# NSA attention: the compressed branch's values in two matmuls and a bank of their own, added to the stored unit by GpSimd

## The chip, the cores and the metric

The kernel runs on one core of one Trainium2 chip. The metric is the device time of one execution in microseconds (us); a change of a few microseconds in some 2300 is looked for. The engines are named as in the profile: PE is TensorE (PEld its weight loads), DVE is VectorE, ACT is ScalarE, POOL is GpSimd, SP is SyncE. Each of them takes its instructions from a queue in a fixed order; semaphores order them against each other.

## The reference

The program is a decoder trunk of four layers on 512 tokens of width 1024: RG-LRU, native sparse attention (NSA), gated linear attention, RG-LRU, each followed by a SwiGLU network. All is float32. The change concerns the NSA layer alone, and in it the sum over three branches at the end:

```
p_c = masked_softmax(lg_c, dist_c >= 0)                      # compressed branch: 31 blocks of keys
o_c = jnp.einsum('bghqn,bngd->bqghd', p_c.astype(vc.dtype), vc)
...
return gi[..., 0:1] * o_c + gi[..., 1:2] * o_s + gi[..., 2:3] * o_w
```

There are 16 heads in 4 groups; a group shares its keys and values, a head has 64 dimensions, and a block of queries has 128 tokens, so there are 4 groups times 4 query blocks = 16 pairs (g, i). Each query sees three branches: compressed (o_c), selected (o_s; with 512 tokens all blocks are selected) and window (o_w).

## The kernel before

The attention stage (function attention, from L957) runs over 32 units: a unit is a group g, a block of queries i and a branch br (0: selected and compressed together, 1: window). The order of the blocks within a group is in NSA_AT["order"]. run() (L1159) steps over the units: it issues the logits of the unit three steps ahead (L1005), some filler matmuls (queries of the last group, and later the output product of the first two groups, L1074), the multiplications of the unit after that by its softmax weights on GpSimd (weights, L1054, the multiply is L1060), and then the values of the present unit (L1086).

In values, the exponentials of each head are transposed by PE into a bank "pt" (L1116) and copied or split from PSUM to SBUF by ScalarE and VectorE (L357 and L358, or L1120, L1122); the product with the values V is accumulated over all key blocks of both branches in one PSUM bank "ob" per pair (g, i) (L1103 to L1106). The products are queued in pend and come out up to four steps late (drain). For the compressed branch, the weights of four heads stand in one 128x128 tile (four heads times 32 blocks): PE transposes it (L1095), ScalarE copies it into the slot pc (L1097), and four matmuls (L1109), one a head, each with the 64 value columns of that head in vcd (zero outside the head's 32 rows), add to the lower 64 partitions of ob.

When the window branch of a pair is finished, store() (L1130) reads ob twice for each of two half rows (ScalarE copies L1136, VectorE adds L1137), which gives the unit's output ov in a slot "o"; then ScalarE and VectorE split it into a high and a low part for the output product (L1143, L1144). The output product of groups 0 and 1 is filler within the attention, that of groups 2 and 3 follows after it (output(4), L329 to L331 with tile "no").

PE's queue in the attention is in the order in which the program is written (manual_schedule). The order of the other engines is made by a planner when the kernel is built: it simulates, with its own costs, which instruction is ready when, and takes the earliest in program order of those ready. PSUM has 8 banks in one pool (bank()); the small SBUF tiles are 54 slots of 128x512 in one pool (slot()). A tile waits until the tile that had its place before has been read for the last time. GpSimd also issues the DMAs that add one weight block to another (L250, L293), in the same queue as its arithmetic.

Of the kernel before, what the change touches and what calls it, by code (L numbers as in the profile page):

```python
# [11 lines left out]
AF = mybir.ActivationFunctionType  # L12
OP = mybir.AluOpType
# [179 lines left out]
class Kernel:  # L193
# [762 lines left out]
    def attention(self, j, kc, kw, qw, V, vcd, gt, os, queries, output):  # L956
        nc, mm = self.nc, self.nc.tensor.matmul  # L957
# [33 lines left out]

        small = lambda s, n=4: self.fixed.tile([128, n], F32, name=self.name(s), tag=s, bufs=4)
        lag, depth = NSA_AT["lag"][0], NSA_AT["depth"][0]
        st, OB, pend, stored = {}, {}, [], []
        LC = [self.fixed.tile([128, 128], F32, name=f"lc{i}") for i in range(4)]
        for x in LC:
            nc.gpsimd.memset(x, 0.0)
# [72 lines left out]
        def drain(n):  # L1070
            while len(pend) > n:
                pend.pop(0)()
# [13 lines left out]
        def values(u, es):  # L1086
            g, i, br = u
            d = st.pop(u)
            L = d["L"]
            if br == 0:  # L1090
                OB[g, i] = self.bank("ob")
            ob = OB[g, i]
            if br == 0:
                b = self.bank("pc")
                nc.tensor.transpose(b[:, 0:128], d["lc"][:, 0:128], self.ident)  # L1095
                pc = self.slot("pc")
                nc.scalar.activation(pc[:, 0:128], b[:, 0:128], AF.Copy)  # L1097

            def product(jt, p):
                v = V[jt, br][:, g * 128:g * 128 + 128]  # L1100
                first, last = br == 0 and jt == 0, br == 1 and jt == i
                if len(p) == 1:
                    mm(ob, lhsT=v.bitcast(F32), rhs=p[0], start=first, stop=last)  # L1103
                else:
                    mm(ob, lhsT=v, rhs=p[0], start=first, stop=False)
                    mm(ob, lhsT=v, rhs=p[1], start=False, stop=last)  # L1106
                if br == 0 and jt == 0:
                    for hh in range(4):
                        mm(ob[0:64, hh * 128:hh * 128 + 128], lhsT=vcd[:, g, hh, :], rhs=pc[:, 0:128], start=False, stop=False)  # L1109

            ne = len(es)
            for jt in range(i + 1):
                b = self.bank("pt")
                for hh in range(4):
                    c = slice(hh * 128, hh * 128 + 128)
                    nc.tensor.transpose(b[:, c], L[hh][:, jt * 128:jt * 128 + 128], self.ident)  # L1116
                if NSA_AT["whole"][g] >> (jt + 4 * br) & 1:
                    p = [self.slot("p")]
                    if (jt + br) % 2:
                        nc.scalar.activation(p[0], b, AF.Copy)  # L1120
                    else:
                        nc.vector.tensor_copy(p[0], b)  # L1122
                else:
                    p = self.split(b, "p")
                pend.append(lambda jt=jt, p=p: product(jt, p))
                drain(depth)
                for _ in range(ne * (jt + 1) // (i + 1) - ne * jt // (i + 1)):
                    es.pop(0)()
            if br == 1:
                def store():  # L1130
                    o = self.slot("o")
                    ov = o[:, 0:256].rearrange("p (b n) -> p b n", n=128)
                    obv = ob.rearrange("p (b two n) -> p b two n", b=2, two=2)
                    for e in range(2):
                        me, ot = slice(e * 64, e * 64 + 64), slice(64 - e * 64, 128 - e * 64)
                        nc.scalar.activation(ov[me], obv[ot, :, e], AF.Copy)  # L1136
                        nc.vector.tensor_tensor(ov[me], obv[me, :, e], ov[me], op=OP.add)  # L1137
                    for b in range(2):
                        k = 2 * g + b
                        if k not in os:  # L1140
                            os[k] = (self.slot("oh", F32R), self.slot("ol", F32R))
                        hi, lo = (t[:, i * 128:i * 128 + 128] for t in os[k])
                        nc.scalar.activation(hi, ov[:, b], AF.Copy)  # L1143
                        nc.vector.tensor_tensor(lo, ov[:, b], hi.bitcast(F32), op=OP.subtract)  # L1144
                    stored.append(u)
                pend[-1] = lambda f=pend[-1]: (f(), store())
# [12 lines left out]
        def run():  # L1159
            for n in range(-lag, N):  # L1160
                es = []
                if n + lag < N:
                    logits(units[n + lag])
                    es = st[units[n + lag]]["exp"]
                fill(NSA_AT["fill"][n % 8])
                if 0 <= n + lag - 1 < N:
                    weights(units[n + lag - 1])
                if n >= 0:
                    values(units[n], es)
                while es:  # L1170
                    es.pop(0)()
                fill(NSA_AT["more"][n % 8] if n >= 1 else NSA_AT["start"][0])
                k = (n + lag) % 8
                if n + lag < 24:
                    for x, t in enumerate(NSA_AT["prep"]):
                        if t == k:
                            prep(units[n + lag][0] + 1, x)
            drain(0)
            for _ in work:
                pass  # L1180
# [290 lines left out]
```

## Time and profile before

| | us |
|---|---|
| median of 3 runs | 2312.25 (2311.42 to 2312.82) |
| the profiled execution's own time | 2310.41 |
| its span, first to last instruction | 2308.7 |
| attention stage in the trace | about 664 to 852 |

Over the span PE is busy 2277.9 us (99%), DVE 1482.1 (64%), ACT 1221.8 (53%) and POOL 346.9 (15%). A share of busy time is a mean over stages that have different limits; the stage around the change has to be read for itself. PE's busy time is modelled with overlapping ends, so a busy PE is not one at its peak. Matmuls on plain float32 appear as two instructions each.

### The profile page before, as it was taken

What the parts mean: (1) busy time and instruction counts of PE and PEld (TensorE: products, weight loads), DVE (VectorE), ACT (ScalarE), POOL (GpSimd) and SP (SyncE); (2) the same over time, 40 slices, a digit from 0 to 9 for tenths busy, and PEclk for the clock granted to TensorE, in tenths of its full rate; (3) what the DMA queues carried; (4) which work ended last, traced back from release to release, by engine and by line L of the source; (5) the groups of instructions that cost most, each with busy time, mean ns of one, the idle gap of its engine ahead of it and who ended that gap; (6) DMA issues with size and microseconds to landing.
All of it is one profiled execution on the core that took longest, in us unless ns stands there. A gap on an engine that the chain in (4) does not pass through costs nothing.

```text
span 2308.7 us, 29405 instructions
## 1 busy us (share of the span) xinstructions
PE 2277.9 (99%) x10898; PEld 1913.5 (83%) x10898; DVE 1482.1 (64%) x2460; ACT 1221.8 (53%) x1971; POOL 346.9 (15%) x413
## 2 busy tenths in 40 slices
PE   8999999999999999999999999999999999999998
PEld 7877888898876778888998887888898887888897
DVE  7887646466289888555466536745466786745555
ACT  5965535353468766444455435625354685635353
POOL 1001101001356531010110000101010000201010
PEclk9999999999999999999999999999999999999999
DMA  9246857452531137666673223958485224857561
GB/s 285 88 119 174 208 133 197 105 151 91 169 83 28 47 87 198 171 151 173 133 218 98 82 74 110 218 137 187 128 201 168 93 79 134 215 147 179 142 140 68
DMA packets 99455, 323.84 MB, mean 140 GB/s; under 512 B 11248, under 2 KB 18032, under 8 KB 99312
## 3 DMA queue, kind: packets, MB, share of 16 engines
q1 hardware_dynamic: 70512, 225.49, 28.9%
q0 software_dynamic: 28800, 96.48, 24.2%
q8 instruction: 85, 1.39, 0.2%
q14 instruction: 58, 0.48, 0.1%
HBM read 316.68 MB, written 5.24 MB: 139 GB/s over the span
## 4 chain that ended last, share of the span: by engine, by line
PE 86%; DVE 8%; ACT 4%; issue 1%; POOL 0%; DMA 0%; SPq 0%; POOLq 0%; DVEq 0%; ACTq 0%
PE pj L330 9%; PE pj L331 9%; PE pj L329 9%; PE b L592 8%; PE b L593 8%; PE b L591 8%; PE t L592 3%; PE t L593 3%; PE t L591 3%; PE lp L329 2%; PE lp L331 2%; PE lp L330 2%; PE at L663 2%; DVE ws L288 1%; DVE L L1032 1%
## 5 line engine op out<-in xcount | busy, mean ns | idle before, releaser
L288 DVE TENSOR_TENSOR ws<-wr,ws 128x1024 fp32r<-128x1024 f32 (+1 forms) x402 | 474.8, 1184 | 414.2 <-ACT ws L287 411.4
L287 ACT ACTIVATE ws<-wr 128x1024 fp32r<-128x1024 f32 (+1 forms) x402 | 409.7, 1021 | 494.0 <-PE pj L331 215.3
L330 PE MATMUL pj<-al,ws 128*128 128x512 f32 (+1 forms) x728 | 278.7, 383 | 0.0
L329 PE MATMUL pj<-ah,ws 128*128 128x512 f32 (+1 forms) x728 | 278.7, 384 | 0.0
L331 PE MATMUL pj<-ah,ws 128*128 128x512 f32 (+1 forms) x728 | 278.4, 382 | 0.0
L288 DVE TENSOR_TENSOR ws<-wc,ws 128x1024 fp32r<-128x1024 f32 (+1 forms) x144 | 163.2, 1133 | 134.7 <-ACT ws L287 133.3
L287 ACT ACTIVATE ws<-wc 128x1024 fp32r<-128x1024 f32 (+1 forms) x144 | 142.2, 988 | 129.2 <-PE pj L331 70.9
L330 PEld LDWEIGHTS pj<-al,ws 128*128 128x128 f32 x728 | 136.9, 188 | 27.1 <-DVE al L358 1.1
L331 PEld LDWEIGHTS pj<-ah,ws 128*128 128x128 f32 x728 | 136.8, 188 | 26.4
L329 PEld LDWEIGHTS pj<-ah,ws 128*128 128x128 f32 x728 | 136.9, 188 | 26.1
L293 POOL DMA_DIRECT2D wc<-wall x88 | 80.4, 923 | 439.6 <-DVE ws L288 431.6
L250 POOL DMA_DIRECT2D wc<-wall x64 | 57.6, 900 | 572.8 <-DMA wc<-wall 231.6
L591 PE MATMUL b<-ws,ph 128*128 128x512 f32 (+1 forms) x384 | 143.4, 373 | 0.0
L592 PE MATMUL b<-ws,xh 128*128 128x512 f32 (+1 forms) x384 | 142.7, 372 | 0.0
L593 PE MATMUL b<-ws,xl 128*128 128x512 f32 (+1 forms) x384 | 142.4, 371 | 0.0
L593 PE MATMUL b<-ws,pl 128*128 128x512 f32 (+1 forms) x384 | 142.4, 371 | 0.0
L592 PE MATMUL b<-ws,ph 128*128 128x512 f32 (+1 forms) x384 | 142.4, 371 | 0.0
L591 PE MATMUL b<-ws,xh 128*128 128x512 f32 (+1 forms) x384 | 142.4, 371 | 0.0
L329 PE MATMUL lp<-xh,ws 128*128 128x512 f32 x320 | 126.1, 394 | 6.6 <-ACT ws L287 6.6
L331 PE MATMUL lp<-xh,ws 128*128 128x512 f32 x320 | 124.4, 393 | 1.1 <-DVE ws L288 1.1
L330 PE MATMUL lp<-xl,ws 128*128 128x512 f32 x320 | 125.4, 392 | 0.0
L541 DVE TENSOR_TENSOR h<-h,pj 128x512 f32<-128x512 f32 x116 | 77.4, 683 | 36.3 <-PE pj L331 36.3
(374 smaller groups left out, 5233.0 us busy)
## 6 DMA issues: line engine op xcount, KB each, us to landing
wr<-wall SPq DMA_DIRECT2D x322, 512.0 KB, 4.2
wc<-wall POOLq DMA_DIRECT2D x104, 512.0 KB, 7.1
wc<-wall SPq DMA_DIRECT2D x40, 512.0 KB, 3.9
wc<-wall POOLq DMA_DIRECT2D x48, 384.0 KB, 6.1
wr<-wall SPq DMA_DIRECT2D x48, 384.0 KB, 3.2
wr<-wall POOLq DMA_DIRECT2D x32, 512.0 KB, 6.2
wc<-wall SPq DMA_DIRECT2D x16, 384.0 KB, 3.1
wr<-wall POOLq DMA_DIRECT2D x16, 384.0 KB, 6.2
```

Source lines behind the costliest of these rows:

```text
L250: self.nc.gpsimd.dma_start(self.raw[i][:, 0:n], self.wall[b][:, 0:n], accum_op=OP.add)
L287: self.nc.scalar.activation(hi, r, AF.Copy)
L288: self.nc.vector.tensor_tensor(lo, r, hi.bitcast(F32), op=OP.subtract)
L293: self.nc.gpsimd.dma_start(whole[:, 0:n], self.wall[self.uses[on][2][0]][:, 0:n], accum_op=OP.add)
L329: mm(ps, lhsT=wh, rhs=x[0], start=first, stop=False)
L330: mm(ps, lhsT=wh, rhs=x[1], start=False, stop=False)
L331: mm(ps, lhsT=wl, rhs=x[0], start=False, stop=last)
L541: nc.vector.tensor_tensor(self.h[m + c], self.h[m + c], banks[c], op=OP.add)
L591: mm(o, lhsT=xh, rhs=wh, start=first and k == 0, stop=False, skip_group_check=True)
L592: mm(o, lhsT=xh, rhs=wl, start=False, stop=False, skip_group_check=True)
L593: mm(o, lhsT=xl, rhs=wh, start=False, stop=k == 3, skip_group_check=True)
L663: nc.tensor.transpose(b[:, i * 128:i * 128 + 128], rows[i][:, c * 128:c * 128 + 128], self.ident)
```

## The change

The four matmuls per pair that added the compressed values to the bank ob are replaced by a function cmp_product: it takes a fresh bank "oc" and makes two matmuls of two heads each (128 value columns instead of 64), one into each 128 columns of the bank. ScalarE copies these 256 columns into the free part of the slot pc, and the copy is kept under OC[g, i]. In store, after the two halves of ov have been formed, GpSimd adds that copy to ov, before ov is split.

```diff
+            def cmp_product():
+                b = self.bank("oc")
+                for e in range(2):
+                    mm(b[:, e * 128:e * 128 + 128], lhsT=vcd[:, g, 2 * e:2 * e + 2, :].rearrange("p h d -> p (h d)"),
+                       rhs=pc[:, 0:128], start=True, stop=True)
+                nc.scalar.activation(pc[:, 128:384], b[:, 0:256], AF.Copy)
+                OC[g, i] = pc[:, 128:384].rearrange("p (b n) -> p b n", n=128)
+
...
                 if br == 0 and jt == 0:
-                    for hh in range(4):
-                        mm(ob[0:64, hh * 128:hh * 128 + 128], lhsT=vcd[:, g, hh, :], rhs=pc[:, 0:128], start=False, stop=False)
+                    cmp_product()
...
                         nc.vector.tensor_tensor(ov[me], obv[me, :, e], ov[me], op=OP.add)
+                    nc.gpsimd.tensor_tensor(ov, ov, OC.pop((g, i)), op=OP.add)
```

## Rows read from the trace of the kernel before

**Rows 1.** Busy time and counts of the engines in two parts of the attention
```profile
core 0: us, PE busy (x) PEld busy (x) DVE busy (x) ACT busy (x) POOL busy (x), PEclk, DMA share, GB/s
664.00:780.00 116.00, 109.67 (x607) 81.24 (x607) 107.37 (x433) 97.49 (x292) 84.58 (x104) 1.00 0.19 47
780.00:852.00 72.00, 70.12 (x396) 56.58 (x395) 65.57 (x226) 50.84 (x147) 31.45 (x44) 0.98 0.25 62
```
**Rows 2.** Waits of DVE and ACT, 664 to 852: total us, times, longest
```profile
DVE pl L358 <- ACT ph L357: 4.3, 10, 1.3
DVE L L1032 <- POOL qq L986: 2.2, 1, 2.2
DVE h L904 <- PE no L331: 0.4, 1, 0.4
DVE lc L1186 <- PE qc L1042: 0.4, 1, 0.4
...
ACT oh L1143 <- DVE o L1137: 4.7, 7, 1.8
ACT o L1136 <- PE ob L1106: 0.8, 1, 0.8
ACT pc L1097 <- POOL qq L986: 0.6, 1, 0.6
ACT ph L357 <- PE pt L1116: 0.5, 2, 0.4
```
**Rows 3.** Chain that ended last, 664 to 853, shares by line, then pieces
```profile
by line: DVE L L1032 11.1%; DVE pl L358 10.3%; ACT L L1046 9.7%; PE pt L1116 6.5%; issue 4.4%; DVE sw L1002 4.3%; DVE ol L1144 4.1%; PE ob L1105 3.3%; PE ob L1106 3.2%; ACT ph L357 3.2%; DVE o L1137 3.0%; PE no L329 2.2%; PE ob L1109 2.2%; 
...
724.77 1.02 PE ob L1109 x8
...
817.77 1.02 PE ob L1109 x8
...
840.03 1.02 PE ob L1109 x8
...
844.07 1.02 PE ob L1109 x8
```
**Rows 4.** Groups of instructions, 664 to 852: count, busy us, mean ns, idle before
```profile
L1109 PE MATMUL ob<-pc,vcd 128*64 128x128 f32 x128 | 17.4, 279 | 0.0
...
L1136 ACT ACTIVATE o<-ob 64x256 f32<-64x256 f32 x32 | 12.1, 379 | 6.0 <-DVE o L1137 4.6 <-PE ob L1106 0.8
L791 ACT ACTIVATE bias<-bias 128x256 f32<-128x256 f32 x12 | 4.4, 406 | 0.1
...
L1060 POOL TENSOR_TENSOR L<-L,sw 128x256 f32<-128x256 f32 x32 | 19.9, 652 | 1.6 <-DVE sc L1065 1.3
L986 POOL TENSOR_TENSOR qq<-qw,qq 64x512 fp32r<-64x512 f32 x12 | 15.4, 1283 | 0.9
...
L1002 DVE TENSOR_TENSOR sw<-sr,gt 128x4 f32<-128x4 f32 x44 | 15.1, 347 | 1.0
```
**Rows 5.** Durations of DVE operations, 664 to 852: ns min/median/max
```profile
L1002 DVE TENSOR_TENSOR sw<-sr,gt x44: 144/166/2727, 667.5 to 837.3; 128x4 f32<-128x4 f32 x44
...
L358 DVE TENSOR_TENSOR pl<-pt,ph x61: 652/681/693, 669.7 to 847.7; 128x512 fp32r<-128x512 f32 x61
```
**Rows 6.** Timeline: a VectorE operation beside a run of GpSimd operations
```profile
825.20 3.46 POOL L1060 TENSOR_TENSOR L<-L,sw 128x384 f32<-128x384 f32 x4
...
825.97 2.73 DVE L1002 TENSOR_TENSOR sw<-sr,gt 128x4 f32<-128x4 f32 x1
```
**Rows 7.** Timeline around the last store and GpSimd's next instructions
```profile
849.04 0.88 POOL L250 DMA_DIRECT2D wc<-wall  x1 [6.38 <-PE no L329]
854.88 0.86 POOL L250 DMA_DIRECT2D wc<-wall  x1 [4.96 <-DMA wc<-wall]
...
850.75 0.43 DVE L1137 TENSOR_TENSOR o<-ob,o 64x256 f32<-64x256 f32 x1
...
851.21 0.51 ACT L1143 ACTIVATE oh<-o 128x128 fp32r<-128x128 f32 x2 [0.49 <-DVE o L1137]
...
851.57 0.30 PEld L329 LDWEIGHTS no<-oh,ws 128*128 128x128 f32 x2 [0.37 <-ACT oh L1143]
```

More of the change, by code (lines that the diff above doesn't have):

```diff
@@ L993, in attention @@
         lag, depth = NSA_AT["lag"][0], NSA_AT["depth"][0]
-        st, OB, pend, stored = {}, {}, [], []
+        st, OB, OC, pend, stored = {}, {}, {}, [], []
         LC = [self.fixed.tile([128, 128], F32, name=f"lc{i}") for i in range(4)]
```

## The prediction

> **What bounds the kernel now.** The page's first part says that PE is busy 99% of the span, and a change that takes matmuls away looks like plain gain. But the change lies wholly in the attention, some 188 us of the 2308.7, so I read that stage by itself: first the busy time by stretch, then who waits for whom, then the chain that ended last.
>
> The stage has two halves that look alike in PE's column and differ in the others [rows 1]. From 664 to 780, PE is busy 109.67 of 116 us, but DVE is busy 107.37 (93%), ACT 97.49 (84%) and POOL 84.58 (73%). From 780 to 852, PE is busy 70.12 of 72 us (97%), DVE 65.57 (91%), ACT 50.84 (71%), POOL 31.45 (44%). PE's clock is at 1.00 and 0.98 of its full level, so it plays no part.
>
> Two engines above 90% cannot both be read from busy shares; the waits decide. Of all idle time of DVE and ACT in the stage, PE ends very little: DVE waits 0.4 us for L331 and 0.4 for L1042, ACT 0.8 for the bank ob and 0.5 for a transposed tile [rows 2], some 2 us in 188. What DVE lacks comes from ACT (4.3 us for the split's high part) and POOL (2.2 us). So PE runs ahead and is stopped by banks that DVE empties; most of the time it is not what is late. The chain says the same: its largest shares are DVE L1032 (11.1%), DVE L358 (10.3%) and ACT L1046 (9.7%), before any line of PE [rows 3].
>
> **Part 1: PE's matmuls.** 64 matmuls of L1109 (16 pairs, 4 each; two instructions a matmul, hence x128 [rows 4]) become 32. The chain shows a group of 8 instructions to take 1.02 us [rows 3], so one costs 0.1275 us. A new one has the same 128 moving columns and 128 weight columns for 64; I take the same price. A group is then 4 x 0.1275 = 0.51 us, and the 16 groups save 16 x 0.51 = 8.2 us of PE. That is the end of the range for the gain. What of it reaches the end? The chain passes through L1109 four times, at 724.77, 817.77, 840.03 and 844.07, and its 2.2% of 189 us (4.1 us) is these four [rows 3]. 4 x 0.51 = 2.0 us. I take -2.0; the bounds are 0 (another line is late at once) and -8.2. The other twelve halvings only let PE stand longer before the next full bank.
>
> **Part 2: GpSimd's add.** 16 additions of 128x256. The nearest row is L1060 with 128x256 elements, 0.652 us; L986 has two full inputs, 512 elements on 64 partitions, and takes 1.283, half of that is 0.64 [rows 4]. I take 0.65, in all 10.4 us on an engine that is not full. Beside its own length it costs DVE something. L1002, an operation on 128x4 elements, has a median of 0.166 us and a maximum of 2.727 [rows 5]; in one place it begins at 825.97 inside a run of four GpSimd multiplications (825.20 to 828.66) and ends with the run [rows 6]. L358, with one input from PSUM, never leaves 0.652 to 0.693 [rows 5]. So small operations with both inputs in SBUF are held by GpSimd, those that read a bank are not. L1002 alone loses 44 x (0.347 - 0.166) = 8.0 us in this way [rows 4, 5] beside 84.58 + 31.45 = 116 us of POOL [rows 1], 0.07 us for each us of POOL; the other lines with this behaviour (L1051, L1066, L1068, L1144, all with SBUF inputs) I put at one and a half times as much again, an estimate, and take 0.18 in all. That is 10.4 x 0.18 = +1.9 us, nearly all on DVE, which is the bound. Bounds: 0 (no such operation falls beside an add) and 10.4 (one stands out every add).
>
> The Trainium skill (SBUF — State Buffer, "Who interferes with whom") says that a VectorE instruction with two SBUF inputs contends with a GpSimd instruction that reads SBUF, and that the one issued first keeps the shared port for the whole instruction. The trace agrees on which operations wait, but the wait of 2.73 us at L1002 outlasts any one of the four multiplications beside it (3.46 us together, so some 0.87 each). By the page's rule an add could hold DVE for at most its own 0.65 us when one arrives in it; by the row an add that is put onto the end of a run holds whoever already waits for the run. The sum above doesn't use the rule.
>
> **Part 3: ScalarE's copy.** 16 copies of 128x256 from PSUM. The nearest rows are L1136 (64x256 from PSUM, 0.379 us) and L791 (128x256, 0.406) [rows 4]; I take 0.38, 16 x 0.38 = 6.1 us more on ACT. ACT's share of the chain is 9.7% for L1046, 3.2% for L357 [rows 3] and smaller lines; I call it a fifth. 6.1 x 0.2 = +1.2 us; bounds 0 and 6.1. The bank oc is held from its first matmul until that copy ends, some 1 to 2 us, 16 times, out of 8 banks for 188 us; I price that at nothing, as DVE's lateness, not the number of banks, sets PE's pace. If that cover is gone, PE would wait one copy, 0.38 us, at some of the 16 places, within the bounds above.
>
> **Part 4: the longer way through store.** Before: DVE L1137, then ACT L1143, then DVE L1144. After: an add on POOL in between. ACT waits 7 times for L1137 in front of L1143 already, 4.7 us in all [rows 2]; there the next thing in ACT's queue was the split, and nothing could go past it. At these the add lengthens the wait by 0.65 us: 7 x 0.65 = 4.6 us of ACT, a fifth of it on the chain: +1.0. Behind the waiting L1143 stand exponentials (L1046) and the splits of pt (L357), which DVE's L358 waits for. Bounds: 0 (the planner finds other work for all) and rival C below. Nobody on PE waits for an inner store but the output product, which follows it by some steps. The slot pc, freed before after L1109, is now kept until store; slots are short where a group's queries are prepared (ACT's L1097 once waited 0.6 us and DVE's L1032 2.2 us for L986, the last reader of another tile [rows 2]). I price that at nothing; the upper bound is another wait of 2.2 us at each of the three changes of group, 6.6.
>
> **Part 5: the last store.** After it nothing covers: L1137 ends at 851.18, ACT follows at 851.21, and PE, which has run out, starts the last rows of the output product at 851.57 after 0.37 us idle [rows 7]. The add, 0.65 us, comes in between, so PE stands 0.65 + 0.05 for a semaphore longer: +0.7. Lower bound 0.3, because PE's earlier work may end later; upper bound in rival B.
>
> **Sum.** -2.0 + 1.9 + 1.2 + 1.0 + 0.7 = +2.8 us. The profiled execution took 2310.41 (span 2308.7 and 1.7 around it), so 2313.2; it lies 1.84 below the median of 2312.25, on which the same +2.8 gives 2315.0. What follows the stage (output product, feed-forward) is moved with it.
>
> **Rivals.**
> A: PE is the bound after all. For it speak 97% busy from 780 on and its 99% overall; against it the waits [rows 2]. All 8.2 us come back, less 0.7 at the last store: 2312.25 - 7.5 = 2304.8.
> B: the last add stands behind a DMA issue in POOL's queue. POOL issues at 849.04, and at 854.88 after a wait of 4.96 us for a DMA [rows 7]. If the planner puts the second issue in front of the last add, that begins at 855.74 and ends at 856.4 where 851.9 was due: 4.5 us more in which PE runs dry, 2315.0 + 4.5 = 2319.5. It decides as soon as that issue is ahead of the add in the queue. Against it: the store is written before what that DMA serves.
> C: ACT stands for POOL at every store. POOL is busy 116 of 188 us, with L1060 in runs of four, 2.6 us for four of 128x256 [rows 1, 4]; an add that arrives at random waits 0.62 x 1.3 = 0.8 us for the run in front and 0.65 for itself, 1.45 x 16 = 23 us. If a third of it comes out at the end (ACT has some 40 us idle) it is +7.7 in place of part 4's +1.0: 2321.7. It decides if the planner believes that POOL is quicker than it is, and so puts L1143 too early; nothing in the rows speaks on that, but ACT's 7 waits for DVE at this very place show that it can be so.
>
> **Chances.** The forecast has 0.47, A with its partial forms 0.22, B 0.11, C 0.20. About 0.2% (4.6 us) can be told from no change: 2307.6 to 2316.9. The forecast's own range, 2311 to 2318, lies mostly inside (0.38) and partly above (0.09); A gives 0.20 faster and 0.02 within; B and C are slower. So faster 0.20, same 0.40, slower 0.40. The range is 2306 to 2322: it takes in C, B and the half of A.
>
> **What would show it.** Right: the group on pc and vcd falls from 128 to 64 instructions and some 8 us of PE's time, but PE's waits for DVE's L358 and L1032 grow; DVE stays busy some 92% of a stage that is as long as before or longer; L1143 is released by POOL at the last store and at some inner ones. Part 2 is wrong if the means of L1002 and L1144 do not rise. The prediction as a whole is wrong if the stage is shorter by 5 us or more (A), or if POOL's add follows a DMA issue at the end (B), or if ACT's waits for POOL before L1143 add up to 10 us or more (C).

## The result, and the profile after

The change makes the kernel slower: 2330.74 us (median of 4 runs, 2329.97 to 2331.59) against 2311.84 for the kernel before in the same comparison (2311.03 to 2312.82). The ratio is 1.0079, with a 95% interval of 1.0067 to 1.0091, that is +18.3 us (15.5 to 21.0). The forecast was 2315.0 with a range up to 2322. In what follows, differences in us are a run's ratio to the kernel before, times 2312.

Work in total hardly changed. PE is busy 2276.2 us (before 2277.9), DVE 1486.3 (1482.1), ACT 1226.9 (1221.8), POOL 358.5 (346.9). The attention, which began at 664 and was over at 852, now lasts until 873; PE stood 8.2 us of these 188, and now stands 30.6 of 209. By stretch (us of the stretch, then busy us and instructions of each engine, clock, DMA share and GB/s), to set beside [rows 1]:

```profile
core 0: us, PE busy (x) PEld busy (x) DVE busy (x) ACT busy (x) POOL busy (x), PEclk, DMA share, GB/s
664.00:780.00 116.00, 98.01 (x513) 74.97 (x513) 97.81 (x392) 91.09 (x276) 78.96 (x99) 0.94 0.16 40
780.00:873.00 93.00, 80.43 (x428) 65.58 (x427) 78.83 (x266) 62.54 (x181) 48.79 (x64) 0.94 0.25 58
```

In the first stretch PE fell from 109.67 busy us to 98.01, DVE from 107.37 to 97.81, and ACT and POOL fell too: in the same 116 us every engine did less. No engine has become full; they all stand more, and PE's granted clock was 0.94 in both parts, where it had been 1.00 and 0.98. The waits say for whom (of ACT, then of DVE, 664 to 873; total us, times, longest; the last two are the kernel before), to set beside [rows 2]:

```profile
ACT oh L1151 <- POOL o L1145: 20.5, 12, 4.1
ACT L L1046 <- DVE m L1032: 19.9, 14, 4.3
ACT pc L1104 <- PE oc L1102: 4.1, 5, 1.4
...
DVE ol L1152 <- ACT oh L1151: 15.1, 11, 3.0
DVE pl L358 <- ACT ph L357: 5.2, 17, 0.7
...
ACT L L1046 <- DVE m L1032: 23.8, 18, 4.3
DVE ol L1144 <- ACT oh L1143: 1.5, 4, 0.4
```

L1151 is the split's high part on ScalarE (L1143 before), L1145 GpSimd's add. The first row takes the place of ACT's 4.7 us for DVE's L1137, and DVE's 15.1 us, before 1.5, hang on it. The new instructions themselves cost about what was expected of them (groups of instructions: count, busy us, mean ns, idle before), to set beside [rows 4]:

```profile
L1145 POOL TENSOR_TENSOR o<-o,pc 128x256 f32<-128x256 f32 x16 | 11.6, 727 | 30.8 <-DVE o L1144 18.1 <-PE ob L1113 8.5 <-PE pt L1123 4.1
...
L1104 ACT ACTIVATE pc<-oc 128x256 f32<-128x256 f32 x16 | 6.0, 374 | 4.1 <-PE oc L1102 4.1
...
L1102 PE MATMUL oc<-pc,vcd 128*128 128x128 f32 x64 | 11.5, 309 | 2.2 <-DVE o L1144 1.2 <-DVE mc L1194 1.0
```

So a 0.73 us operation made ScalarE wait 1.7 us on average and 4.1 at most. GpSimd for its part stood 30.8 us in front of its adds. In 7 of the 16 places the add came straight after multiplications (L1060), 0.67 to 2.84 us after VectorE's sums were ready; ScalarE's waits at these 7 make up 16.8 of the 20.5 us. The chain that ended last, between 694 and 699.5, shows one such wait (start, us, what):

```profile
by line: POOL L L1060 62.5%; issue 13.0%; POOL o L1145 12.5%; DVE ol L1152 6.2%; ACT oh L1151 5.8%; POOL kk L978 3.8%
...
693.93 0.90 POOL L L1060 x2
694.84 0.67 issue
695.50 0.83 POOL L L1060
696.33 0.21 POOL kk L978
696.54 1.71 POOL L L1060 x3
698.25 0.69 POOL o L1145
698.94 0.02 issue
698.97 0.32 ACT oh L1151
```

The unit's two halves were summed when VectorE's L1144 of 694.94 ended at 695.37. The add starts at 698.21, because softmax multiplications (L1060) and a key's low part (L978) are ahead of it in GpSimd's queue; ScalarE stands from 694.91 to 698.97, with exponentials next in its queue. VectorE's low part (L1152) waits 2.96 us for the split, VectorE's L1032 stands behind that, and PE, released by L1032, has been idle 2.91 us at 700.72.

A later one shows a wait that reaches PE by way of ScalarE alone. The timeline of POOL, ACT and PE around 860, and then PE's busy us and clock in short stretches:

```profile
853.82 6.69 POOL L1060 TENSOR_TENSOR L<-L,sw 128x384 f32<-128x384 f32 x8 [1.72 <-DVE sw L1002]
860.47 0.72 POOL L1145 TENSOR_TENSOR o<-o,pc 128x256 f32<-128x256 f32 x1
...
858.20 0.39 ACT L1104 ACTIVATE pc<-oc 128x256 f32<-128x256 f32 x1
861.22 0.51 ACT L1151 ACTIVATE oh<-o 128x128 fp32r<-128x128 f32 x2 [2.64 <-POOL o L1145]
861.64 0.26 ACT L1097 ACTIVATE pc<-pc 128x128 f32<-128x128 f32 x1
861.79 0.59 ACT L357 ACTIVATE ph<-pt 128x512 fp32r<-128x512 f32 x1
...
859.60 0.60 PE L1123 MATMUL pt<-ident,L 128*128 128x128 f32 x4
862.43 0.79 PE L1113 MATMUL ob<-ph,v 128*128 128x512 f32 x1 [2.24 <-ACT ph L357]
863.75 1.05 PE L1102 MATMUL oc<-pc,vcd 128*128 128x128 f32 x4
864.60 1.06 PE L1123 MATMUL pt<-ident,L 128*128 128x128 f32 x4
```

```profile
860.00:862.00 2.00, 0.20 (x2) 1.00 0.70 248
862.00:864.00 2.00, 1.57 (x4) 0.59 0.00 0
864.00:866.00 2.00, 2.00 (x10) 0.56 0.08 16
866.00:868.00 2.00, 2.00 (x12) 1.00 0.64 246
```

GpSimd works off eight multiplications from 853.82, the add comes out at 861.19, ScalarE has stood 2.64 us, the split of the transposed probabilities (L357) that was behind it in the queue begins at 861.79, and PE has been idle 2.24 us when its product starts. The granted clock, 1.00 until then, is 0.59 and 0.56 in the next two stretches, near the lower of its two levels (1.2 GHz, where 2.4 is full), and PE does the two matmuls of L1102, four instructions, in 0.85 us from their start to the next.

The four longest idle times of PE in the stage lie elsewhere:

```profile
700.72 1.12 PE L1111 MATMUL ob<-p,v 128*128 128x512 f32 x2 [2.91 <-DVE m L1032]
...
726.60 0.58 PE L1029 MATMUL qk<-kk,qq 128*128 128x288 f32 x1 [2.79 <-DVE mc L1194]
...
749.92 2.08 PE L1111 MATMUL ob<-p,v 128*128 128x512 f32 x2 [2.52 <-DVE m L1032]
...
805.14 1.11 PE L1123 MATMUL pt<-ident,L 128*128 128x128 f32 x4 [2.75 <-DVE m L1032]
```

Each ends 1.6 to 2.3 us after ScalarE has waited for an add (until 698.97, 724.33, 748.22 and 803.52), the 2.24 us above 1.2 us after it. The next longest, 2.05 us at 790.81, follows no such wait. In the kernel before, PE's longest idle time in the stage is 1.3 us.

### The profile page after: what moved, and what is told of

The parts are those of the page before. It is cut to its first block, busy times and chain, and to the rows that moved or that the text cites. A ratio compares the mean times of both kernels' runs of the same rounds, so it can differ in the third digit from the quotient of the medians.

```text
span 2329.6 us, 29280 instructions
## 1 busy us (share of the span) xinstructions
PE 2276.2 (98%) x10834; PEld 1916.3 (82%) x10834; DVE 1486.3 (64%) x2460; ACT 1226.9 (53%) x1987; POOL 358.5 (15%) x429
## 4 chain that ended last, share of the span: by engine, by line
PE 86%; DVE 6%; ACT 4%; POOL 2%; issue 1%; DMA 0%; POOLq 0%; SPq 0%; DVEq 0%; ACTq 0%
PE pj L330 9%; PE pj L331 9%; PE pj L329 9%; PE b L592 8%; PE b L593 8%; PE b L591 8%; PE t L592 3%; PE t L593 3%; PE t L591 3%; PE lp L329 2%; PE lp L331 2%; PE lp L330 2%; PE at L663 2%; DVE ws L288 1%; POOL L L1060 1%
## 5 line engine op out<-in xcount | busy, mean ns | idle before, releaser
L330 PEld LDWEIGHTS pj<-al,ws 128*128 128x128 f32 x728 | 136.9, 188 | 27.1 <-DVE al L358 1.1
```

Of the source, the lines that this page charges most:

```text
L330: mm(ps, lhsT=wh, rhs=x[1], start=False, stop=False)
```

## The experiments

Each run changes the kernel before or the change by the lines shown (... stands for lines left out). Two theories stood at the start. Q: the add stands in GpSimd's queue, and ScalarE, and after it VectorE and PE, stand in order behind the split that waits for it. W: the wider matmuls, the new bank and ScalarE's copy cost the time. Later a third: P: GpSimd's extra work as such, with its hold on VectorE's small operations.

**e1: VectorE adds.**
```diff
-                    nc.gpsimd.tensor_tensor(ov, ov, OC.pop((g, i)), op=OP.add)
+                    nc.vector.tensor_tensor(ov, ov, OC.pop((g, i)), op=OP.add)
```


> The change with one word different: VectorE, not GpSimd, adds the compressed values to the stored unit. Theory Q (the add stands in GpSimd's queue behind runs of softmax multiplications, and ScalarE and VectorE stand in order behind it): no wait of L1151 for GpSimd is left, VectorE gets 16 x 0.35 = 5.6 us more work, and the time goes back to 2308 to 2316 us. Theory W (the new bank, the wider matmuls and ScalarE's copy cost the time): stays at 2326 or more.

Measured 2319.97 us, ratio 1.0031 (1.0020 to 1.0041), +7.2. The waits for GpSimd at the split are gone, and 11 us of the 18 with them. But the time is above what Q expected. Its add on VectorE:

```profile
L1145 DVE TENSOR_TENSOR o<-o,pc 128x256 f32<-128x256 f32 x16 | 8.3, 516 | 0.1
```

Against e2 below (-1.6) that is +8.8 us for 8.3 us of work on VectorE. ScalarE's split still waits there, now for VectorE's add (9.0 us, against 2.8 for VectorE's sums in e2), so what the work and what the waiting cost are not told apart.

**e2: no add.** The compressed branch is computed and copied, but left out of the output.
```diff
-                    nc.gpsimd.tensor_tensor(ov, ov, OC.pop((g, i)), op=OP.add)
+                    OC.pop((g, i))
```


> The change without the add: the compressed branch's values are computed and copied but left out of the output. It shows what the matmuls, the bank oc and ScalarE's copy are worth by themselves. Theory Q: 2306 to 2313 us (PE's gain on the path, 2 to 5 us, less ScalarE's copy). Theory W: 2325 or more.

2311.34 us, ratio 0.9993 (0.9984 to 1.0003), -1.6. W falls: matmuls, bank and copy together cost nothing. The whole loss comes with the add. A free add would have left a gain of 1.6 us, no more than this measurement can tell from nothing.

**e3: the operation alone.** The four matmuls of before stay, zero is a tile of zeros, made once.
```diff
...
                         nc.vector.tensor_tensor(ov[me], obv[me, :, e], ov[me], op=OP.add)
+                    nc.gpsimd.tensor_tensor(ov, ov, zero[:, None, :].to_broadcast([128, 2, 128]), op=OP.add)
```


> The kernel before with its four matmuls a pair, and one GpSimd operation more in store, which adds a tile of zeros to the stored unit at the place where the change has its add. Theory Q: nearly the whole loss is here, 2325 to 2333 us, with ScalarE's split waiting for GpSimd some 20 us in all. Theory W: 2313 to 2316, the operation's own 0.7 us at the last store and a little contention.

2333.53 us, ratio 1.0089 (1.0074 to 1.0104), +20.6: the loss without any of the rest of the change, the longer life of the slot pc included. Its waits of ACT, and GpSimd's operation:

```profile
ACT oh L1146 <- POOL o L1140: 27.1, 13, 4.7
...
L1140 POOL TENSOR_TENSOR o<-o,zero 128x256 f32<-128x256 f32 x16 | 11.6, 727 | 29.5 <-DVE o L1139 11.6 <-PE pt L1118 10.8 <-PE ob L1107 6.8
```

**e10: the same operation, but nobody reads its output.** It tells Q from P: as e3, with the sum written to the unused half of the slot o.
```diff
-                    nc.gpsimd.tensor_tensor(ov, ov, zero[:, None, :].to_broadcast([128, 2, 128]), op=OP.add)
+                    nc.gpsimd.tensor_tensor(o[:, 256:512].rearrange("p (b n) -> p b n", n=128), ov, zero[:, None, :].to_broadcast([128, 2, 128]), op=OP.add)
```


> As e3 (the kernel before with one GpSimd operation more in store), but the operation writes to a free part of the slot that nothing reads, so the split doesn't wait for it. GpSimd does the same 16 operations of the same size and order class. Theory Q: 2312 to 2317 us, against 2333.5 of e3. Theory P: 2328 or more.

2313.48 us, ratio 1.0006 (0.9996 to 1.0016), +1.4. GpSimd does the same work (first row, 12.2 us, in e3 11.6), it still waits for VectorE's sums, and the split waits for VectorE as in the kernel before (second row, the same 4.7 us in 7 times as in [rows 2]):

```profile
L1140 POOL TENSOR_TENSOR o<-o,zero 128x256 f32<-128x256 f32 x16 | 12.2, 759 | 13.3 <-DVE o L1139 8.5 <-PE ob L1107 3.5 <-PE qk L1032 1.2
...
ACT oh L1146 <- DVE o L1139: 4.7, 7, 1.4
```

Between e3 and e10 lies one dependence in the program, and 19 us. What comes with the dependence is in these 19 us too: GpSimd stands 13.3 us in front of its operation in e10 and 29.5 in e3, and the planner puts some instructions of ScalarE and VectorE in another order (GpSimd's order is the same). The shares of these were not separated. P falls: 12 us more of GpSimd's work in this place cost 1.4 us, within -0.9 to 3.7.

**e4 and e5: the split later.** The split (L1151, L1152 of the change) becomes a function finish, which the loop calls one step later (e4) or three (e5).
```diff
-                    for b in range(2):
-                        k = 2 * g + b
...
-                    stored.append(u)
+                    def finish():
+                        for b in range(2):
...
+                        stored.append(u)
+                    late.append(finish)
...
```


> The change, with the split of the stored unit (ScalarE, VectorE) written one step of the loop later, so that the planner has other work for ScalarE while GpSimd adds. Theory Q: most of the loss goes, 2310 to 2318 us, though GpSimd does the same 16 adds; ScalarE's waits for GpSimd at the split fall below 6 us. If instead GpSimd's extra 11.6 us of work and its contention with VectorE are the cost (theory P), it stays at 2325 or more.

> The change with the split of the stored unit written three loop steps later instead of one. If ScalarE's standing for GpSimd is what costs (theory Q), its waits at the split fall from 12.6 us to 5 or less, and the time falls from 2321 to 2311 to 2316 us, near the kernel without the add (2311.3). If GpSimd's 11.6 us of work and its hold on VectorE cost by themselves (theory P), it stays at 2319 or more.

e4: 2321.09 us, ratio 1.0035 (1.0022 to 1.0048), +8.1; ScalarE's wait at the split fell to 12.6 us (11 times). That takes away more than half of the loss, by order alone, with all 16 adds on GpSimd, but time and wait both stayed above what Q expected. e5: 2323.53, ratio 1.0048 (1.0033 to 1.0063), +11.1, which by the expectation lies on P's side; it is e10, run later, that decides against P. Its waits at the split are 7.0 us, but 6.2 of these are one, at the end of the stage. First the wait, then GpSimd's, ScalarE's and PE's timeline there:

```profile
ACT oh L1153 <- POOL o L1145: 7.0, 4, 6.2
...
853.74 0.88 POOL L250 DMA_DIRECT2D wc<-wall  x1 [6.78 <-PE ob L1113]
861.06 0.86 POOL L250 DMA_DIRECT2D wc<-wall  x1 [6.44 <-DMA wc<-wall]
861.62 1.05 POOL L1145 TENSOR_TENSOR o<-o,pc 128x256 f32<-128x256 f32 x1
...
862.70 0.51 ACT L1153 ACTIVATE oh<-o 128x128 fp32r<-128x128 f32 x2 [6.17 <-POOL o L1145]
...
863.74 0.98 PE L329 MATMUL no<-oh,ws 128*128 128x512 f32 x2 [4.37 <-ACT oh L1153]
864.51 0.63 PE L330 MATMUL no<-ol,ws 128*128 128x512 f32 x1
```

This is rival B, in another kernel than the one it was written for: the last adds stand behind a DMA issue that waits 6.44 us for a transfer, and PE is idle 4.37 us. What the rest of e5's loss is made of was not separated. The output product of groups 0 and 1 starts later there, at 774.7 (768.8 in the change, 757.1 before), and from 780 to 880 the granted clock was 0.94, where it was 0.98 in e4.

**e9: the two cures put together.** GpSimd adds in groups 0 and 2, with the split three steps later; VectorE adds in groups 1 and 3, with the split at once.
```diff
+                    at_once = g == 1 or g == 3
+                    (nc.vector if at_once else nc.gpsimd).tensor_tensor(ov, ov, OC.pop((g, i)), op=OP.add)
...
+                    if at_once:
+                        finish()
+                    else:
+                        late.append((self.step_n + 3, finish))
...
```


> The change with the best of e1 and e5: in groups 0 and 2 GpSimd adds and the split follows three steps later; in groups 1 and 3, whose last stores the output product waits for, VectorE adds and the split follows at once. Theory Q (every wait of ScalarE for GpSimd costs, in the middle as at the end): ScalarE's waits at the split below 2 us, 2312 to 2317 us: half of e1's price of 8.6 us over the kernel without the add, none of the end of e5. Theory P (GpSimd's work itself costs): 2318 or more.

2316.81 us, ratio 1.0015 (1.0005 to 1.0024), +3.5. ScalarE waits 2.2 us for GpSimd in all, VectorE has 3.9 us of adds. Of the versions of the change that compute the whole output this is the best, and it is still not faster than the kernel before.

**e6: the matmuls alone.** What PE's saving is worth, without the copy and the add; the compressed branch is left out of the output.
```diff
-                nc.scalar.activation(pc[:, 128:384], b[:, 0:256], AF.Copy)
-                OC[g, i] = pc[:, 128:384].rearrange("p (b n) -> p b n", n=128)
...
-                    nc.gpsimd.tensor_tensor(ov, ov, OC.pop((g, i)), op=OP.add)
```


> Two matmuls a pair into a bank of their own, and nothing else of the change: no copy by ScalarE, no add; the compressed branch's values are left out of the output. It prices PE's saving alone. If PE is not the bound (the prediction's reading): 2308.5 to 2311.5, 2 to 3 us below before. If PE is the bound: 2303 to 2306, all 8 us.

2308.76 us, ratio 0.9984 (0.9975 to 0.9994), -3.7 (-5.8 to -1.4). PE is not the bound in the sense of rival A. The saving on PE was larger than assumed: the next instruction follows the start of the four of L1102 after 0.36 us in 11 of the 16 groups (789.97 to 790.33 below) and after 6.8 us in all 16 together, against 16 x 1.02 = 16.3 before, so 9.5 us. About two fifths came out.

```profile
789.97 0.61 PE L1102 MATMUL oc<-pc,vcd 128*128 128x128 f32 x4
790.33 0.47 PE L329 MATMUL no<-oh,ws 128*128 128x512 f32 x1
```

**e7 and e8: VectorE relieved, PE paying.** e8 is the kernel before with 12 more tiles that are not split, e7 is e5 with the same.
```diff
-    "whole": [21, 145, 0, 0],
+    "whole": [23, 147, 2, 2],
```


> e5 with one more tile of probabilities per pair (jt 1 of the first branch, 12 tiles in all) kept whole in float32: PE pays 12 x 0.4 = 4.8 us out of what the change freed, VectorE is spared 12 splits of 0.68 = 8.2 us. If VectorE is the bound: 4 to 7 us below e5, and possibly below both kernels (2306 to 2311). If PE is: 3 us or more above e5.

> The kernel before with the same 12 tiles kept whole: control for e7. If VectorE alone is the bound: 2306 to 2309; if PE is close behind it (97% busy from 780 on): 2311 to 2315, because here PE has no slack to pay with.

e7: 2328.14 us, ratio 1.0067 (1.0052 to 1.0082), 4.4 us above e5; e8: 2319.68, ratio 1.0032 (1.0020 to 1.0044), +7.4. e7 lies where it was expected if PE is the bound, e8 above both of its ranges. Taking 7.7 us of splits off VectorE (L358, 40.9 to 33.2 us) for some 5 us more on PE (an estimate, 12 x 0.4) makes the stage longer, so "VectorE is the bound" is too simple. In e8 DVE waits more than twice as long for the ScalarE halves of splits as in [rows 2] (10.0 us against 4.3), and ACT 34.1 us for the logits' maxima against 23.8 before:

```profile
ACT L L1046 <- DVE m L1032: 34.1, 21, 5.3
...
DVE pl L358 <- ACT ph L357: 10.0, 16, 1.4
```

Why these grew was not tried: the planner makes another order for the whole stage when 12 instructions go.

## Why the prediction was wrong

**The step that failed is part 4,** the longer way through store, put at +1.0 us. e2 and the change differ by the add (and by the longer life of the slot pc; e3 loses as much without it): 18.3 + 1.6 = 19.9 us. Of these e10 gives 1.4 to GpSimd's work and its hold on VectorE (part 2). The last store gives 0.8: PE's weight load waits 1.15 us there, before 0.37 [rows 7]. That leaves some 18 us for part 4. Three things in its working were wrong.

First, the wait was taken as the add's own length, 0.65 us, at the 7 stores where ScalarE already waited. In the trace it waits 12 times and 1.7 us on average, most of it where multiplications are ahead of the add. POOL's busy share of 73% in the first half was in [rows 1]; I used it for the queue only in rival C.

Second, the wait was multiplied by a fifth, ScalarE's share of the chain. That share was read for more work on an engine, not for standing. A wait at the head of a queue that runs in order stops everything behind it: exponentials that GpSimd needs, splits that VectorE and then PE need. Against 20.5 us of waiting some 18 came out at the end, where the fifth would give 4; in e3 it was 19 for 27.1. Part of these 18 us may have come by way of PE's clock (last section).

Third, rival C named this mechanism, its place and its waiting time (23 us; measured 20.5), and then let a third through, as "ACT has some 40 us idle". Idle time in other places did not take up the waits at this one. With its whole 23 us, and the sum's other terms, C would have given 2312.25 + 1.8 + 23 = 2337, too high by 6 but on the right side. That its 23 us lie so near the 20.5 is partly luck: C had 16 waits of 1.45 us, the trace has 12 of 1.7. C's condition, a planner that believes GpSimd quicker than it is, was not tried. Its sign came (10 us or more of such waits); the sign for the forecast, VectorE busy some 92%, did not: 176.6 of 209 us are 85%.

**The other steps.** Part 1 (-2.0): right in kind; e6 gives -3.7 (its interval holds -2.0), from a larger saving (9.5 us on PE instead of 8.2). Part 2 (+1.9): e10 gives +1.4, but its interval reaches from -0.9 to 3.7, and the mechanism is not shown. The mean of L1002 is 0.423 us in the change, 0.347 before [rows 4], but 0.341 in e10 with the same GpSimd work; that of the low part (L1144 before) fell from 0.420 to 0.328 in the change and rose to 0.488 in e10. The prediction had asked for both to rise. Part 3 (+1.2): e2 less e6 is +2.1, with intervals that overlap. Part 5 (+0.7): right, +0.8.

**What bounded the kernel.** That PE is not what is late in most of the stage was right, and rival A with its whole saving is refuted by e6. That VectorE is the bound is half right at most: 8.3 us of work on it, with the waits it brought, cost 8.8 us (e1), but relieving it by 7.7 us at some 5 of PE's cost 7.4 (e8). PE, VectorE and ScalarE each wait for the other two over short distances, and no run found slack in them that could be spent. Rival B did not occur in the change (its last adds, at 871.07, waited for VectorE), but did in e5.

## What to carry to other kernels

When an operation is put into a chain between two engines, price the queue that it joins, not its duration: here 0.73 us became 1.7 us of waiting at 12 of 16 places, since the third engine, busy 61% of the stage, mostly had other work ahead of it. A wait at the head of a queue in order is not to be multiplied by that engine's share of the chain; ask what is queued behind it. And to tell the cost of an operation from the cost of waiting for it, let it write where nobody reads (e10): the same work was +1.4 us, with the dependence +20.6.

## What the runs showed of the hardware that was not expected

Matmul instructions of 128 weight columns came at the same pace as those of 64: single starts inside a group are 0.11 us apart in e6 and in the kernel before. A group of eight took 1.02 us to the next instruction [rows 3] and a group of four 0.36, less than half, because of its ends: the first step in a group of eight is 0.16 us, and the step from its last instruction to the next line 0.20, against 0.03 in 13 of e6's 16 groups. Why these steps differ was not tried.

Short waits of PE cost more than their length. After 2.24 us idle at 862.43 the granted clock fell to 0.56 to 0.59, and PE's matmuls ran at about half rate until some 866. The four longer idle times shown with the result lie beside such stretches too: the granted clock was 0.50 (the lower level) from 702 to 705, 726 to 732, 750 to 753 and 805 to 811, and PE was busy 17.3 of these 18 us. Over the whole stage it was 0.94 in the changed kernel and 0.97 in e3, against 1.00 and 0.98 in the two parts before [rows 1]. By these means the clock lacked 0.06 x 209 = 12.5 us of full speed in the change, 0.03 x 212 = 6.4 in e3 and 0.02 x 72 = 1.4 before. So, as an estimate, at most some 11 of the change's 18 us and 5 of e3's 21 can have come by way of the clock. Each time it fell in such an idle time or within 1.2 us of its end, so the traces show it following the waits; how much of it reached the end was not separated.
